# Key/value banks of a hybrid decoder block: one ScalarE copy ahead of the rest of the evacuation, and a later load of the feed-forward gate vector

## The chip, the core and the metric

The kernel runs on one core of a Trainium2 chip. TensorE (PE in the profile) multiplies matrices into PSUM banks of 128 x 512 single-precision numbers; VectorE (DVE), ScalarE (ACT) and GpSimd (POOL) do the rest. All transfers between the chip's memory and SBUF are issued by SyncE (SP), one after the other. Each engine runs its own instructions strictly in the order in which the program lists them, and waits for other engines at semaphores.

The metric is the device time of one execution in microseconds, the median of several runs. Before the change it is 2741.42 us (three runs, 2739.41 to 2742.02).

## The reference

One decoder layer on 2048 tokens of width 1024. Two mixers, sliding-window attention and a chunkwise mLSTM, work on one common projection, and a SwiGLU feed-forward part follows:

```python
h = modulate(rms_norm(x, g_pre_mix[l]), shift_m, scale_m)
proj = h @ w_in[l]
q_a, k_a, v_a, q_m, k_m, v_m, o_m, i_m, f_m, g_a, g_m = jnp.split(proj, split_points, axis=-1)
q_a = rope(q_a.reshape(B, S, N_Q_HEADS, HEAD_DIM), positions)      # 8 heads of 64
k_a = rope(k_a.reshape(B, S, N_KV_HEADS, HEAD_DIM), positions)     # 2 heads of 64
...
i_pre = i_m + b_if[l][:MLSTM_HEADS]                                # 4 and 4 columns
f_pre = f_m + b_if[l][MLSTM_HEADS:]
...
x = x + gate_m[:, None, :] * rms_norm(mix, g_post_mix[l])
h2 = modulate(rms_norm(x, g_pre_ffn[l]), shift_f, scale_f)
ff = (jax.nn.silu(h2 @ w_ffn_gate[l]) * (h2 @ w_ffn_up[l])) @ w_ffn_down[l]
x = x + gate_f[:, None, :] * rms_norm(ff, g_post_ffn[l])
```

`rope` turns each head's two halves of 32: `[t1*cos - t2*sin, t2*cos + t1*sin]`. The attention of a block of 128 queries sees its own 128 keys and the 128 before, so the kernel keeps, next to each token tile's values, their difference from the values of the tile before.

## The kernel before

**Blocks and stages.** The 2048 tokens are four blocks of 512 (`NBLK`), two blocks a superblock (`NSB`), four tiles of 128 tokens a block (`NT`). A superblock projects queries and keys/values of its first block (`q_kv(b0)`), the mLSTM values of both blocks (`vm(b0)`, `vm(b1)`), then `q_kv(b1)`; the other columns of the projection follow in pairs (`pair_parts`), with a scheme of seven instead of eight products. Attention and mLSTM run as streams beside these matmuls, and so do the preparation of the next block's h (`hprep`, `hsums`) and the modulation (`ada_stream`). After both superblocks' outputs comes the feed-forward part (`program2`): for each half of the tokens `gate_up`, then `down`.

**Precision.** Every product is made of three matmuls: weights and activations are split into a rounded part (a ScalarE cast, L259 or L1348) and a rest (a VectorE subtraction, L260 or L1349). So each part of the weights needs ScalarE, then VectorE, before TensorE can use it.

**Order.** The program text gives an order by priority, with streams interleaved by a clock that the program keeps itself (`now`, `spawn`, `tick`). The order on each engine is laid out when the program is built: it is opened with `schedule_with_timeline_sim=True`, so a scheduler plays through estimated times, issues on each engine what is ready, and gives out buffers as they come free. Once built, each engine's order is fixed.

**Banks and buffers.** The projections accumulate in `acc`, four banks. `token_group` takes all four at once, one per token tile, and calls `evac` for tile 0 to 3 as each one's last matmul is issued. A bank is free when the last instruction that reads it is done. The temporaries of the evacuations are tiles `tx`: nine buffers of one size, shared by rope, the modulation's loads, the convolutions and others.

**The query evacuation.** `rope` (L746 on) copies the bank into a `tx` tile on ScalarE (L751), multiplies by cosine and sine on VectorE (L759 to L761), then subtracts and adds (L762, L763). `q_stream` later transposes the result, splits it (L772, L773) and sends it to `at_d` in memory (L775).

**The key/value evacuation** (`evac_kv`, L800 on). The bank's 264 columns are 128 of keys, 128 of values, 8 of gates. VectorE adds the gate biases from the bank (L801, L802); ScalarE copies the values into `va` (L804); VectorE subtracts the last tile's values `v_last` from the bank (L805); ScalarE copies the new values into `v_last` (L806); SyncE sends both (L808, L810); then `rope` copies the keys from the bank (L751) and turns them, with its last add (L763) on GpSimd. `k_stream` transposes and splits the keys (L793, L794) and sends them to `at_d` (L797), from where the attention loads them (L898 to L903).

**The border.** The feed-forward part works in memory that the mixers gave back: `open_ffn` closes their pools and opens `fpool`. The first thing in `program2` is `load_gg` (L1809): it takes the first tile of that pool, 128 x 1024, and loads the gate vector `gg_f_d`, which `gated` multiplies with in `down` (L1652). Shortly after, `rest_of_hc` loads eight pieces of the feed-forward's h from `hc_d` (L1426) into tiles `w` and makes the rests of two operands of them (L1429). The last rows of `x` after the mixers leave by L579.

Of the kernel before, what the change touches and what calls it, by code (L numbers as in the profile page):

```python
# [10 lines left out]
F32 = mybir.dt.float32  # L11
# [4 lines left out]
ALU = mybir.AluOpType  # L16
# [3 lines left out]
P = 128  # L20
S = 2048
D = 1024
KD = D // P
TB = 512
NT = TB // P
# [6 lines left out]
HQ, HKV, HD = 8, 2, 64  # L32
# [39 lines left out]
def decoder_block(ctx: ExitStack, tc: tile.TileContext, a: dict, out: bass.AP, dbg=None):  # L72
    nc = tc.nc
    V, A, G, T = nc.vector, nc.scalar, nc.gpsimd, nc.tensor
# [18 lines left out]
    def nm(s):  # L93
        uid[0] += 1
        return f"{s}{uid[0]}"
# [4 lines left out]
    def mix_tile():  # L100
        return ps_mix.tile([P, 512], F32, tag="mix", name=nm("mix"))

    def tx(shape, dtype=F32):
        return tpool.tile(shape, dtype, tag="tx", name=nm("tx"), bufs=9)
# [48 lines left out]
    b_if = const.tile([P, 8], F32, name="b_if")  # L153
# [52 lines left out]
    def transpose(o, i):  # L206
        now[0] += 110.0
        k = i.shape[0]
        T.transpose(o, i, ident[:k, :k])  # L209

    def spawn(gen, delay=0.0):
        st = [now[0] + delay, gen, False]
        streams.append(st)
        return st
# [473 lines left out]
    AT_K, AT_V, AT_N = 2 * 512, 2 * 512 + 4 * P, 2 * 512 + 6 * P  # L688
# [12 lines left out]
    gt = kvp.tile([P, NT, 36], F32, name="gt")  # L701
    V.memset(gt, 0.0)
    v_last = kvp.tile([P, P], F32, name="v_last")
# [23 lines left out]
    at_d = [tc.dram_tile([P, AT_N], F32, name=f"at_d{i}") for i in range(S // P)]  # L727
# [8 lines left out]
    def superblock(sb):  # L736
        b0, b1 = 2 * sb, 2 * sb + 1
        R = {}
# [4 lines left out]
            return lhs  # L743


        def rope(ps, heads, b, t):  # L746
            sin, cos = tables[sb]
            t += (b % 2) * NT
            W = heads * HD
            raw = tx([P, W])  # L750
            A.copy(raw, ps[:, :W])  # L751
            src = raw.rearrange("p (h u f) -> p h u f", u=2, f=32)
            cb = cos[:, t, :].unsqueeze(1).to_broadcast([P, heads * 2, 32])
            sb_ = sin[:, t, :].unsqueeze(1).to_broadcast([P, heads, 32])
            y = tx([P, W])
            z = tx([P, W])
            zz = z.rearrange("p (h u f) -> p h u f", u=2, f=32)
            yy = y.rearrange("p (h u f) -> p h u f", u=2, f=32)
            V.tensor_tensor(y.rearrange("p (h f) -> p h f", f=32), raw.rearrange("p (h f) -> p h f", f=32), cb, op=ALU.mult)  # L759
            V.tensor_tensor(zz[:, :, 0, :], src[:, :, 1, :], sb_, op=ALU.mult)  # L760
            V.tensor_tensor(zz[:, :, 1, :], src[:, :, 0, :], sb_, op=ALU.mult)  # L761
            V.tensor_tensor(yy[:, :, 0, :], yy[:, :, 0, :], zz[:, :, 0, :], op=ALU.subtract)  # L762
            (G if heads == HKV else V).tensor_tensor(yy[:, :, 1, :], yy[:, :, 1, :], zz[:, :, 1, :], op=ALU.add)  # L763
            return y

        def q_stream(b, t, y):
            yield L_ROPE
            pt = mix_tile()
            for j in range(GQ):
                transpose(pt[:, j * P:(j + 1) * P], y[:, j * P:(j + 1) * P])  # L770
            hi, lo = tx([P, 512], F32R), tx([P, 512], F32R)
            A.activation(hi, pt, AF.Copy, scale=HD ** -0.5)  # L772
            V.scalar_tensor_tensor(lo, pt, HD ** -0.5, hi.bitcast(F32), op0=ALU.mult, op1=ALU.subtract)  # L773
            for i, q in enumerate((hi, lo)):
                nc.sync.dma_start(at_d[b * NT + t][:, i * 512:(i + 1) * 512], q.bitcast(F32))  # L775
# [1 line left out]
        R["qk"] = []  # L777

        def evac_q(b):
            return lambda t, ps: R["qk"].append(spawn(q_stream(b, t, rope(ps, HQ, b, t))))  # L780

        def load_kv():
            raw = raw_tile([KD, 264])
# [4 lines left out]
        def k_stream(n, y):  # L788
            yield L_ROPEK
            pt = mix_tile()  # L790
            transpose(pt[:, :P], y)
            kk = tx([P, 2, P], F32R)
            A.copy(kk[:, 0, :], pt[:, :P])  # L793
            V.tensor_tensor(kk[:, 1, :], pt[:, :P], kk[:, 0, :].bitcast(F32), op=ALU.subtract)  # L794
            for n_, u in ((n, 1), (n + 1, 0)):
                if n_ < S // P:
                    nc.sync.dma_start(at_d[n_][:, AT_K:AT_V].rearrange("p (i u k) -> p i u k", i=2, u=2)[:, :, u, :], kk.bitcast(F32))  # L797

        def evac_kv(b):
            def evac(t, ps):  # L800
                V.tensor_tensor(gt[:, t, 0:4], ps[:, 256:260], b_if[:, 0:4], op=ALU.add)  # L801
                V.tensor_tensor(gt[:, t, 32:36], ps[:, 260:264], b_if[:, 4:8], op=ALU.add)  # L802
                va = tx([P, 2, P])
                A.copy(va[:, 0, :], ps[:, 128:256])  # L804
                V.tensor_tensor(va[:, 1, :], ps[:, 128:256], v_last, op=ALU.subtract)  # L805
                A.copy(v_last, va[:, 0, :])  # L806
                n = b * NT + t
                nc.sync.dma_start(at_d[n][:, AT_V + P:], va[:, 1, :])  # L808
                if n + 1 < S // P:
                    nc.sync.dma_start(at_d[n + 1][:, AT_V:AT_V + P], va[:, 0, :])  # L810
                R["qk"].append(spawn(k_stream(b * NT + t, rope(ps, HKV, b, t))))
            return evac

        def q_kv(b):
# [516 lines left out]
    F = {}  # L1331
# [3 lines left out]
    def unit():  # L1335
        if "pool" not in F:
            return tm([P, TB])
        return F["pool"].tile([P, TB], F32, tag="w", name=nm("w"), bufs=16)
# [209 lines left out]
    def gate_up(b2):  # L1548
        late = None
        for p in range(NP):  # L1550
            g = {}

            def done_g(qd, t, in_psum, g=g):
                g[qd] = unit()
                A.activation(g[qd], t, AF.Sigmoid)
                V.tensor_tensor(g[qd], t, g[qd], op=ALU.mult)

            def done_u(qd, t, in_psum, p=p, g=g):
                V.tensor_tensor(g[qd], t, g[qd], op=ALU.mult)

                names = {"11": "11", "12": "21", "21": "12", "22": "22"}
                F["a", names[qd]] = g[qd]
                if qd != "12":
                    nc.sync.dma_start(as_d[b2][:, IDX[names[qd]], p, :], g[qd])
                    return
                g["all"] = {n: F.pop(("a", n)) for n in ("11", "12", "21", "22")}

            def a_sums(p=p, g=g):
                a_ = g["all"]
                s1_, s2_, s4_ = unit(), unit(), unit()  # L1570
                V.tensor_tensor(s1_, a_["21"], a_["22"], op=ALU.add)
                V.tensor_tensor(a_["21"], a_["11"], a_["21"], op=ALU.subtract)
                V.tensor_tensor(s2_, s1_, a_["11"], op=ALU.subtract)
                V.tensor_tensor(s4_, a_["12"], s2_, op=ALU.subtract)
                for n, t_ in (("S1", s1_), ("S3", a_["21"]), ("S2", s2_), ("S4", s4_)):
                    nc.sync.dma_start(as_d[b2][:, IDX[n], p, :], t_)

            gp, up = (list(pair_parts(w, p * 256, done, unit, unit, mix_tile)) for w, done in ((wg, done_g), (wu, done_u)))
            load, sums = down_weights(p)
            if F.get("late") is not None and p == 0:  # L1580
                def a_step():
                    if F["late"]:
                        F["late"].pop(0)()

                for part in gp + up:
                    part.after = a_step
            yield from gp[:2]
            if b2 + p == 0:
                yield lambda: rest_of_hc(0)
            if late:  # L1590
                yield late
            yield from gp[2:4]
            if b2 + p == 0:
                yield lambda: rest_of_hc(1)
            if b2 == 0:
                yield load
            yield from gp[4:] + up[:3]
            if b2 == 0:
                yield sums
            yield from up[3:]  # L1600
            late = a_sums
            if b2 == 0 and 1 <= p <= NT:
                yield lambda t=p - 1: norm_rows(NBLK - 1, t)
        yield late
# [193 lines left out]
    def program():  # L1798
# [7 lines left out]
        yield lambda: next(phase2)  # L1806
        yield from items[last:]

    def load_gg():  # L1809
        F["gg"] = F["pool"].tile([P, D], F32, name="gg_f")  # L1810
        nc.sync.dma_start(F["gg"], gg_f_d)

    def program2():
        yield load_gg
        for b2 in range(NB2):
            yield from gate_up(b2)
            yield from down(b2)

    phase2 = run2(program2())
    for _ in run2(program(), {i: lambda i=i: ada_raws.update({c0: load_ada(c0, n) for c0, n, _ in ADA[ADA_AHEAD[i - 1]:ADA_AHEAD[i]]}) for i in (1, 2)}):  # L1820
        pass
# [29 lines left out]
```

## Time and profile before

| | |
|---|---|
| median of 3 runs | 2741.42 us (2739.41 to 2742.02) |
| profiled execution | 2741.79 us, of which the span from the first to the last instruction is 2740.1 us |
| mean granted TensorE clock | 0.988 |
| VectorE busy | 1995.3 us (73%) |
| ScalarE busy | 1292.4 us (47%) |
| memory traffic | 513.99 MB, mean 188 GB/s |

In a list of waits, a row reads: engine and line that waited, after the arrow the engine and line it waited for, then the total, how often, and the longest. In a timeline a row gives start, duration, engine, line, operation, output and inputs, shapes and how many were merged; the bracket holds the idle time of the engine just before and what ended it. In the chain of waits, which is followed back from the last instruction, a row gives start, length and what ran. Tiles are named without their numbers: `acc` and `mix` are PSUM banks, `whi`, `wlo` and `hl` split weights, `big` large buffers. Busy time by stages, in us, around the four key/value projections:

```
stage (us)      TensorE busy   VectorE busy   granted clock
60 to 110           38.72          45.19          0.93
110 to 140          28.67          24.18          1.00
140 to 190          50.00          23.82          1.00
190 to 240          39.68          43.72          0.90
740 to 800          50.23          51.13          0.92
800 to 880          80.00          52.77          0.99
880 to 960          71.12          68.52          0.94
```

The four key/value projections end near 86, 208, 772 and 896 us.

### The profile page before, as it was taken

The numbers are of one execution on the slowest core, as the hardware profiler recorded it, in microseconds if no ns is written. First come the engines' busy times: TensorE is split into PE (matmuls) and PEld (weight loads), VectorE is DVE, ScalarE is ACT, GpSimd is POOL, SyncE is SP. The second block draws the span as 40 slices with busy tenths as digits, with TensorE's granted clock in tenths as the row PEclk, the third lists the DMA queues.
The fourth block names the chain that finished last, engine by engine and source line by source line (L and its number), as shares of the span: only waits on it lengthen the run. The fifth ranks groups of instructions, "written<-read, shape, count | busy, mean of one in ns | idle before, by whom it ended". The sixth has DMA issues, their size and how long they took to land.

```text
span 2740.1 us, 35791 instructions
## 1 busy us (share of the span) xinstructions
PE 2646.6 (97%) x12310; PEld 2139.0 (78%) x12310; DVE 1995.3 (73%) x3922; ACT 1292.4 (47%) x2542; POOL 158.6 (6%) x205
## 2 busy tenths in 40 slices
PE   6898999999989899999998999999999999999998
PEld 4666788888876668888887888888877888888886
DVE  7959877767785988876586767776677766766466
ACT  5646644445754564344563433334554333333444
POOL 2010002100101000110000000000000000000000
PEclk9999999999999999999999999999999999999999
DMA  6655445687674545568755654446675323324566
GB/s 247 232 173 166 139 142 174 212 330 257 218 239 126 199 154 159 185 219 304 255 195 197 198 179 161 147 157 204 208 261 192 116 98 102 108 97 141 183 214 215
DMA packets 355223, 513.99 MB, mean 188 GB/s; under 512 B 25297, under 2 KB 213837, under 8 KB 349921
## 3 DMA queue, kind: packets, MB, share of 16 engines
q1 hardware_dynamic: 355040, 511.71, 56.3%
q8 instruction: 97, 1.59, 0.2%
q14 instruction: 86, 0.70, 0.1%
HBM read 358.17 MB, written 145.06 MB: 184 GB/s over the span
## 4 chain that ended last, share of the span: by engine, by line
PE 80%; DVE 7%; DMA 6%; issue 4%; ACT 2%; SPq 0%; POOL 0%; DVEq 0%; POOLq 0%; ACTq 0%
PE acc L204 57%; PE mix L204 22%; PE mix L209 2%; DVE hl L1349 1%; DVE tm L428 1%; DMA raw<-in_w_ffn_down_dram 1%; DMA big<-big 1%; DMA tx<-in_w_ada_dram 1%; DMA big<-g_d 1%; ACT hl L1348 1%; DVE wlo L260 0%; DMA raw<-as_d 0%; DMA at<-at_d 0%; DMA big<-in_x_dram 0%; ACT tm L941 0%
## 5 line engine op out<-in xcount | busy, mean ns | idle before, releaser
L204 PE MATMUL acc<-big,hl 128*128 128x512 f32 x3936 | 949.5, 395 | 14.9 <-ACT tx L751 13.1
L204 PEld LDWEIGHTS acc<-big,hl 128*128 128x128 f32 x3936 | 735.8, 189 | 184.3 <-ACT tx L751 13.5
L1348 ACT CAST hl<-raw 128x512 fp32r<-128x512 f32 x732 | 440.2, 621 | 488.4 <-PE acc L204 226.7
L1349 DVE TENSOR_TENSOR hl<-raw,hl 128x512 fp32r<-128x512 f32 x732 | 497.9, 696 | 195.9 <-ACT hl L1348 195.4
L204 PE MATMUL acc<-whi,big 128*128 128x512 f32 (+1 forms) x1280 | 382.7, 378 | 22.8 <-ACT tx L751 15.0
L204 PE MATMUL mix<-big,hl 128*128 128x512 f32 x1232 | 334.0, 393 | 8.1 <-DVE big L1429 7.0
L204 PEld LDWEIGHTS acc<-whi,big 128*128 128x128 f32 x1280 | 234.9, 190 | 72.5 <-ACT tx L751 15.9
L204 PEld LDWEIGHTS mix<-big,hl 128*128 128x128 f32 x1232 | 231.7, 188 | 59.9 <-DVE big L1429 7.5
L204 PE MATMUL acc<-wlo,big 128*128 128x512 f32 (+1 forms) x640 | 240.6, 378 | 4.6 <-DVE wlo L260 4.5
L204 PE MATMUL acc<-hl,hl 128*128 128x512 f32 x1008 | 237.0, 393 | 4.3 <-DVE hl L1349 2.4
L204 PEld LDWEIGHTS acc<-hl,hl 128*128 128x128 f32 x1008 | 187.0, 188 | 49.6 <-DVE hl L1349 7.9
L204 PE MATMUL mix<-hl,hl 128*128 128x512 f32 x792 | 183.2, 391 | 2.4 <-ACT hl L1348 1.6
L204 PEld LDWEIGHTS mix<-hl,hl 128*128 128x128 f32 x792 | 147.9, 188 | 36.8 <-ACT hl L1348 3.5
L260 DVE TENSOR_TENSOR wlo<-raw,whi 128x1024 fp32r<-128x1024 f32 (+1 forms) x96 | 110.3, 1149 | 76.1 <-ACT whi L259 70.1
L204 PE MATMUL acc<-big,whi 128*128 128x512 f32 x512 | 155.0, 391 | 1.2 <-ACT whi L259 1.2
L259 ACT CAST whi<-raw 128x1024 fp32r<-128x1024 f32 (+1 forms) x96 | 94.3, 984 | 120.6 <-PE acc L204 116.1
L204 PEld LDWEIGHTS acc<-wlo,big 128*128 128x128 f32 x640 | 122.7, 192 | 28.1 <-DVE wlo L260 6.2
L475 POOL TENSOR_TENSOR rs<-ms,nhalf 128x1 f32<-128x1 f32 (+1 forms) x56 | 42.1, 764 | 1650.6 <-DVE ms L473 1518.7
L204 PE MATMUL acc<-hcT2h,hl 128*128 128x512 f32 x352 | 118.1, 396 | 1.5 <-ACT w L1492 1.5
L204 PE MATMUL mix<-hcT4h,hl 128*128 128x512 f32 x352 | 117.3, 394 | 0.0
L204 PEld LDWEIGHTS acc<-big,whi 128*128 128x128 f32 x512 | 95.6, 188 | 21.2 <-ACT whi L259 1.7
L204 PE MATMUL acc<-big,wlo 128*128 128x512 f32 x256 | 96.4, 392 | 0.1
(333 smaller groups left out, 3392.7 us busy)
## 6 DMA issues: line engine op xcount, KB each, us to landing
raw<-in_w_in_dram SPq DMA_DIRECT2D x48, 1024.0 KB
as_d<-w SPq DMA_DIRECT2D x154, 256.0 KB
raw<-as_d SPq DMA_DIRECT2D x70, 512.0 KB
raw<-in_w_ffn_gate_dram SPq DMA_DIRECT2D x22, 1024.0 KB
raw<-in_w_ffn_up_dram SPq DMA_DIRECT2D x22, 1024.0 KB
raw<-ws_d SPq DMA_DIRECT2D x40, 512.0 KB
tx<-in_w_ada_dram SPq DMA_DIRECT2D x64, 256.0 KB
y_d<-tm SPq DMA_DIRECT2D x64, 256.0 KB
```

The costliest lines, as they stand in the source:

```text
L204: T.matmul(o, lhsT=lhsT, rhs=rhs, start=start, stop=stop, skip_group_check=resumed)
L209: T.transpose(o, i, ident[:k, :k])
L259: A.copy(hv, src)
L260: V.tensor_tensor(lv, src, hv.bitcast(F32), op=ALU.subtract)
L428: V.scalar_tensor_tensor(acc, raw[:, k, :], c_, acc, op0=ALU.mult, op1=ALU.add)
L475: G.tensor_tensor(r[:, :n], ms[:, :n], nhalf[:, :n], op=ALU.pow)
L1348: A.copy(v(hi), src)
L1349: V.tensor_tensor(v(lo), src, v(hi).bitcast(F32), op=ALU.subtract)
```

## The change

In the key/value evacuation one ScalarE copy takes all 264 columns of the bank into a `tx` tile, now 392 columns wide. Everything else reads that tile: rope the keys, VectorE the values (the difference goes into columns 264 to 391) and the gate columns. The order becomes rope, difference, `v_last` (now a VectorE copy), gate additions. Both transfers leave from that one tile, so a token tile takes four `tx` buffers (this one, two of rope, one of `k_stream`) instead of five. Rope's last addition is on VectorE for keys too. The query evacuation makes the same copy as before, outside `rope`.

In the feed-forward part the place of the gate vector is still taken first, by `place_gg`; its load is issued after the first `gate_up`, ahead of the first `down`.

```diff
-        def rope(ps, heads, b, t):
+        def rope(raw, heads, b, t):
             sin, cos = tables[sb]
             t += (b % 2) * NT
             W = heads * HD
-            raw = tx([P, W])
-            A.copy(raw, ps[:, :W])
+            raw = raw[:, :W]
...
-            (G if heads == HKV else V).tensor_tensor(yy[:, :, 1, :], yy[:, :, 1, :], zz[:, :, 1, :], op=ALU.add)
+            V.tensor_tensor(yy[:, :, 1, :], yy[:, :, 1, :], zz[:, :, 1, :], op=ALU.add)
             return y
...
         def evac_q(b):
-            return lambda t, ps: R["qk"].append(spawn(q_stream(b, t, rope(ps, HQ, b, t))))
+            def evac(t, ps):
+                raw = tx([P, 512])
+                A.copy(raw, ps)
+                R["qk"].append(spawn(q_stream(b, t, rope(raw, HQ, b, t))))
+            return evac
...
         def evac_kv(b):
             def evac(t, ps):
-                V.tensor_tensor(gt[:, t, 0:4], ps[:, 256:260], b_if[:, 0:4], op=ALU.add)
-                V.tensor_tensor(gt[:, t, 32:36], ps[:, 260:264], b_if[:, 4:8], op=ALU.add)
-                va = tx([P, 2, P])
-                A.copy(va[:, 0, :], ps[:, 128:256])
-                V.tensor_tensor(va[:, 1, :], ps[:, 128:256], v_last, op=ALU.subtract)
-                A.copy(v_last, va[:, 0, :])
+                raw = tx([P, 392])
+                A.copy(raw[:, :264], ps[:, :264])
+                v, dv = raw[:, 128:256], raw[:, 264:392]
                 n = b * NT + t
-                nc.sync.dma_start(at_d[n][:, AT_V + P:], va[:, 1, :])
+                y = rope(raw, HKV, b, t)
+                V.tensor_tensor(dv, v, v_last, op=ALU.subtract)
+                V.tensor_copy(v_last, v)
+                V.tensor_tensor(gt[:, t, 0:4], raw[:, 256:260], b_if[:, 0:4], op=ALU.add)
+                V.tensor_tensor(gt[:, t, 32:36], raw[:, 260:264], b_if[:, 4:8], op=ALU.add)
+                nc.sync.dma_start(at_d[n][:, AT_V + P:], dv)
                 if n + 1 < S // P:
-                    nc.sync.dma_start(at_d[n + 1][:, AT_V:AT_V + P], va[:, 0, :])
-                R["qk"].append(spawn(k_stream(b * NT + t, rope(ps, HKV, b, t))))
+                    nc.sync.dma_start(at_d[n + 1][:, AT_V:AT_V + P], v)
+                R["qk"].append(spawn(k_stream(n, y)))
             return evac
...
-    def load_gg():
+    def place_gg():
         F["gg"] = F["pool"].tile([P, D], F32, name="gg_f")
+
+    def load_gg():
         nc.sync.dma_start(F["gg"], gg_f_d)
 
     def program2():
-        yield load_gg
+        yield place_gg
         for b2 in range(NB2):
             yield from gate_up(b2)
+            if b2 == 0:
+                yield load_gg
             yield from down(b2)
```

More of the change, by code (lines that the diff above doesn't have):

```diff
@@ L1807, in program @@
         yield from items[last:]
+    def place_gg():
+        F["gg"] = F["pool"].tile([P, D], F32, name="gg_f")
     def load_gg():
-        F["gg"] = F["pool"].tile([P, D], F32, name="gg_f")
         nc.sync.dma_start(F["gg"], gg_f_d)
     def program2():
-        yield load_gg
+        yield place_gg
         for b2 in range(NB2):
             yield from gate_up(b2)
+            if b2 == 0:
+                yield load_gg
             yield from down(b2)
```

## The prediction, made before the result was known

> **What bounds the kernel now.** I read the busy times of the page first, then the list of waits for TensorE alone, then the timeline of TensorE around each of the long waits.
>
> ```profile
> PE 2646.6 (97%) x12310; PEld 2139.0 (78%) x12310; DVE 1995.3 (73%) x3922; ACT 1292.4 (47%) x2542; POOL 158.6 (6%) x205
> ```
>
> TensorE works in 2646.6 of 2740.1 us, so whatever shortens the program must come out of the 93.5 us in which it stands, or out of stretches in which it works slowly. The waits (total, times, longest):
>
> ```profile
> PE acc L204 <- ACT tx L751: 28.0, 5, 8.6
> ...
> PE mix L204 <- DVE big L1429: 7.0, 1, 7.0
> ...
> PE acc L204 <- DVE wlo L260: 4.5, 3, 2.1
> ```
>
> The first is the copy at L751 that empties a PSUM bank. The timeline (start, duration, then in brackets the idle time and who ended it) shows where:
>
> ```profile
> 94.63 0.80 PE L204 MATMUL acc<-whi,big 128*128 128x512 f32 x1 [8.55 <-ACT tx L751]
> ...
> 216.49 4.96 PE L204 MATMUL acc<-big,hl 128*128 128x512 f32 x12 [8.34 <-ACT tx L751]
> ...
> 221.32 2.98 PE L204 MATMUL acc<-big,hl 128*128 128x512 f32 x12
> ...
> 760.86 0.39 PE L204 MATMUL acc<-whi,big 128*128 128x264 f32 x1 [2.54 <-ACT tx L751]
> ...
> 780.86 0.79 PE L204 MATMUL acc<-whi,big 128*128 128x512 f32 x1 [3.90 <-ACT tx L751]
> ...
> 900.55 4.35 PE L204 MATMUL acc<-big,hl 128*128 128x512 f32 x12 [4.71 <-ACT tx L751]
> ```
>
> Four of the five (8.55, 8.34, 3.90, 4.71; together 25.5) stand at the end of the key/value projection of one block of 512 tokens: it fills all four banks of the pool, and the next projection can't start until a bank is free. The fifth (2.54) is a query bank, which the change leaves as it is. There is a second price: after such a wait 12 matmuls take 4.96 or 4.35 instead of 2.98, a tail of 1.98 or 1.37 us in which the array runs slowly. After 3.90 the first matmul is slow too (0.79), after 2.54 it is not (0.39).
>
> Why the bank is held so long is told by the chain of waits that ended last (start, length, what):
>
> ```profile
> 93.88 0.21 DVE tx L805
> ...
> 94.12 0.30 ACT v_last L806
> 94.42 0.17 ACT tx L751
> ...
> 94.63 7.23 PE acc L204 x24
> ```
>
> ScalarE does L804, L806, L751 in this order. L806 must wait for the subtraction at L805, and VectorE gets to that late. The bank is free only after the last of them, though ScalarE's first read of it came much earlier:
>
> ```profile
> 89.62 0.29 ACT L804 COPY tx<-acc 128x128 f32<-128x128 f32 x1
> ...
> 211.58 0.26 ACT L804 COPY tx<-acc 128x128 f32<-128x128 f32 x1
> ...
> 774.63 0.28 ACT L804 COPY tx<-acc 128x128 f32<-128x128 f32 x1
> ...
> 895.99 0.25 ACT L804 COPY tx<-acc 128x128 f32<-128x128 f32 x1
> ```
>
> **The change, part by part: the single copy.** It takes the place of L804 as the first ScalarE instruction of a tile and frees the bank alone. No row shows a copy of 264 columns; the nearest are 128 and 512:
>
> ```profile
> L751 ACT COPY tx<-acc 128x512 f32<-128x512 f32 x16 | 9.0, 591 | 10.4 <-DVE tx L761 6.7 <-issue 3.4 <-PE acc L204 0.2
> ...
> L804 ACT COPY tx<-acc 128x128 f32<-128x128 f32 x16 | 4.2, 265 | 2.7 <-DMA at_d<-tx 2.5 <-DVE tx L761 0.2
> ```
>
> On the line between them it is 265 + (136/384) x 326 = 380 ns (bounds 265 and 591). I leave it at L804's time, because what stands ahead of L804 on ScalarE (casts and the h tiles) isn't touched, and add 0.04 us to the matmul. New starts: 89.62 + 0.42 = 90.04, against 94.63: 4.6 gained. 211.58 + 0.42 = 212.0, against 216.49: 4.5. At 775.05 TensorE is still at its transposes (they end at 780.86 - 3.90 = 776.96), so all 3.9 go. 895.99 + 0.42 = 896.4 against 900.55: 4.1. Sum 17.1. The wait of the third vanishes and that of the fourth falls to 0.6, so their slow tails go too: 1.4 each by the 900.55 row, 2.8. The first two still stand 3.96 and 3.85 us, as long as the 3.90 that was slow; I leave their tails. Gain so far 19.9. Bounds: the copies come no earlier than L751 does now (0), or as soon as the bank is full (25.5 and all four tails).
>
> The Trainium skill ("TensorE: Matmul & The Clock Gate", section "What's actually happening") says that about 3.4 us without work halve the clock until the array has been busy as long again. The 2.54 and the 3.90 above agree; by its window half a microsecond less of the first two waits would save some 3 us more.
>
> **What VectorE takes over.** Per tile it gets the add of L763 from POOL and the copy of `v_last` from ScalarE; the two gate adds and the subtraction only change their source.
>
> ```profile
> L805 DVE TENSOR_TENSOR tx<-acc,v_last 128x128 f32<-128x128 f32 x16 | 4.5, 284 | 0.6 <-ACT tx L804 0.6
> ...
> L1122 DVE COPY tx<-hist 128x3 f32<-128x3 f32 x21 | 4.0, 197 | 0.0
> L762 DVE TENSOR_TENSOR tx<-tx,tx 128x64 f32<-128x64 f32 x16 | 3.8, 236 | 0.0
> ```
>
> The add is as L762, 236 ns of which some 90 overlap the neighbour; the copy lies between 197 (three columns) and 284. About 0.3 us a tile, 1.2 a block. That would be free where VectorE has room, but it has none here (columns: window, width, PE, PEld, DVE, ACT, POOL, clock, DMA, GB/s):
>
> ```profile
> 90.00:100.00 10.00, 5.37 (x17) 4.32 (x18) 9.93 (x33) 4.82 (x13) 1.15 (x2) 0.66 0.70 239
> ...
> 210.00:220.00 10.00, 3.51 (x8) 2.81 (x9) 10.00 (x27) 4.77 (x12) 0.70 (x1) 0.52 0.78 253
> ```
>
> I charge the first two blocks 1.2 each, 2.4. In return rope no longer stands behind L751. Rope's five instructions and the gate adds now wait for one copy; behind the gate adds stand only the gates (L830 on), needed much later by the mLSTM.
>
> **What is late next.** TensorE comes earlier to work whose inputs hang on transfers (chain of waits again):
>
> ```profile
> 109.85 7.16 DMA tx<-in_w_ada_dram
> ...
> 125.74 5.23 DMA tx<-in_w_ada_dram
> ...
> 898.50 8.75 DMA big<-big
> ...
> 911.56 2.57 PE acc L204 x10
> ```
>
> Between 110 and 131 (125.74 + 5.23) the chain goes through loads for the modulation, whose times TensorE doesn't set: I take half of the first block's 4.6 back, 2.3 (bounds 0 and 4.6). In the fourth the sums T1 and T3 land at 907.25 (898.50 + 8.75) whatever TensorE does, and it needed split weights behind them at 911.56: 2.0 back of 5.5. The bank copies are worth 19.9 - 2.4 - 2.3 - 2.0 = 13.2.
>
> **The gate vector.** The chain at the border to the feed-forward part, and what SyncE issued there:
>
> ```profile
> 1440.27 4.38 DMA x<-tm
> ...
> 1444.66 0.32 SPq L1811
> ...
> 1445.04 4.55 DMA w<-hc_d
> ...
> 1450.36 2.93 PE mix L204 x6
> ```
>
> ```profile
> 1440.87 0.38 SPq L1515 DMA_DIRECT2D raw<-in_w_ffn_gate_dram  x1
> ```
>
> The load at L1811 goes into memory that the last `x` rows still leave, waits 3.3 us for that, and behind it on SyncE's queue stand the eight loads of `hc_d` for which L1429 and then TensorE wait (7.03). Without it the first may issue at 1441.3 instead of 1445.04: 3.7 earlier at best. It then meets the weight load issued at 1440.87. Sizes:
>
> ```profile
> raw<-in_w_ffn_gate_dram SPq DMA_DIRECT2D x1, 1024.0 KB
> w<-hc_d SPq DMA_DIRECT2D x8, 256.0 KB
> ...
> gg_f<-gg_f_d SPq DMA_DIRECT2D x1, 512.0 KB
> ```
>
> Now 512 + 256 KB take from 1444.66 to 1449.59, 4.93; if 1024 + 256 KB took that pace from 1440.87, the load would land at 1449.1, 0.5 earlier. I take 2.0 between 0.5 and 3.7 (0 if its own buffer waits for the same rows). The moved load costs SyncE 0.32 us and one transfer at the start of the down projection, near 1838; its first reader comes at 1996.5, so it is hidden by 150 us of matmuls:
>
> ```profile
> L1625 SPq DMA_DIRECT2D raw<-as_d x84: 319/320/456, 1838.1 to 2717.0; - x84
> ```
> ```profile
> L1652 DVE TENSOR_TENSOR w<-w,gg_f x24: 679/684/693, 1996.5 to 2705.5; 128x512 f32<-128x512 f32 x24
> ```
>
> The Trainium skill ("DMA: Bandwidth & Descriptors", section "Issuing engines are not separate DMA queues") has all transfers share the same 16 engines, which speaks for the 0.5; by that the sum would be 1.5 worse.
>
> **Sum.** 13.2 + 2.0 = 15.2. The profiled execution took 2741.79 (2740.1 of it span), the median of the runs is 2741.42, 0.4 below. 2741.8 - 15.2 - 0.4 = 2726.
>
> **Rivals.** First, the copies move up to where the banks fill. For it: a tile now needs four `tx` buffers instead of five, so a copy may find one sooner; against it: ScalarE was busy with earlier work until 89.6. All 25.5, four tails (1.98 + 3 x 1.4 = 6.2) and 3.7 at the border: 35.4, giving 2706.
>
> Second, the gain is given back: VectorE was full and stays the bound, TensorE starts sooner and stands later at the split weights and attention loads. For it speaks that the chain into 94.63 is VectorE work; against it, that TensorE waits for split weights (L260) 4.5 us in all today. Only the third block's 3.9 + 1.4 less 2.4 is left, and nothing at the border: 2738.5.
>
> Third, slower: the copy of the fourth tile takes the buffer of the first, which is held until two transfers from it have landed, and ScalarE, in order, stands on it with the weight casts behind. Such a transfer has taken
>
> ```profile
> 778.70 6.69 DMA at_d<-tx
> ```
>
> At the first block: VectorE reaches tile 0 at 93.9, has rope and difference (six instructions of some 0.2) done at about 95.2, the buffer comes at 101.9. TensorE, started at 90.04 with a tail of 2, has used the three free banks (18 matmuls of 2.98/12 us) by 96.5: it stands 5.4 and pays a tail of 1.8 again, 7.2 against 4.6 gained. Four times 2.6, plus 2.4, less 2.0 at the border: 10.8 slower, 2752. It decides once that copy comes later than about 99. Against it: nine buffers, four tiles of them needed at once, and only 2.5 us of L804 waiting for such a transfer today.
>
> That the change doesn't do what it says would be L804's place slipping: the order on each engine is laid out at build time from estimated times, so the new copy can be put behind other casts. That ends as the second rival.
>
> **How the numbers follow.** Forecast 0.47, more gain 0.18, given back 0.20, slower 0.15. No change means within 0.2%, 5.5 us, about what a measurement of this kernel can tell: 2735.9 to 2746.9. Of "given back" 0.05 falls below, 0.13 inside, 0.02 above; of "slower" 0.04 inside, since it need not strike all four blocks. Faster 0.47 + 0.18 + 0.05 = 0.70, same 0.17, slower 0.13. The range runs from 2706 to 2746, which leaves out most of the slower case and the tip of the first; the forecast's own is 2718 (nothing charged or taken back, 3.7 at the border) to 2734 (half of 15.2).
>
> **What would show it.** TensorE's waits for the key/value copy down to some 8 us in all and near 90, 212 and 896, none at 776; the copy in 0.38; no wait of ScalarE for VectorE in the evacuation; the wait at the border near 5 us. Wrong would be: waits of the same size behind split weights, `at_d` or `big<-big` a few us later (second rival), or ScalarE standing on `tx` before the fourth copy (third).

## The result, and the profile after the change

| kernel | median, us | runs | ratio to the kernel before, 95% interval |
|---|---|---|---|
| before | 2743.14 | 8 | |
| after the change | 2733.48 | 8 | 0.9962 [0.9952, 0.9971] |

The change is faster by 0.38% of 2743, 10.4 us; the two profiled executions have spans of 2740.1 and 2729.8, 10.3 apart. The forecast was 15.2 faster. The kernel before has five more runs here than ahead of the prediction, so its median is 2743.14 where it was 2741.42.

The profile after, first the busy times of the page, then the list of TensorE's waits (total us, times, longest):

```profile
PE 2641.6 (97%) x12310; PEld 2133.7 (78%) x12310; DVE 1999.4 (73%) x3954; ACT 1287.9 (47%) x2510; POOL 153.2 (6%) x189
```
```profile
PE acc L204 <- ACT tx L805: 9.8, 6, 4.2
...
PE acc L204 <- DVE hl L1354: 6.9, 7, 1.9
PE mix L204 <- DVE big L1434: 6.0, 1, 6.0
...
PE acc L204 <- ACT w L1497: 4.4, 4, 1.3
PE acc L204 <- DVE wlo L260: 4.1, 3, 2.2
PE acc L204 <- ACT tx L781: 4.0, 3, 2.2
PE acc L204 <- ACT tx L827: 3.4, 3, 1.9
```

L805 is the new copy, L781 the query copy that was part of L751. Together they cost TensorE 13.8 us where L751 cost 28.0, so 14.2 of waiting went. The busy time fell by 5.0 (2646.6 to 2641.6), the slow matmuls after the long waits. But other waits grew. L1354 (the rests of split operands, L1349 before) went from 2.8 to 6.9, L1497 (the copy of a bank in the feed-forward part, L1492 before) from 1.5 to 4.4, and L827 (the copy of a bank with mLSTM values) is new with 3.4. From the list of before:

```profile
PE acc L204 <- DVE hl L1349: 2.8, 4, 1.1
...
PE acc L204 <- ACT w L1492: 1.5, 2, 1.0
```

The wait at the border to the feed-forward part (L1434, L1429 before) fell by 1.0.

Where the 10.3 came from is seen by setting the n-th matmul of one trace beside the n-th of the other; both have 12310. Inside a stage their order differs, so the difference means something only where both traces are in step again, as from 300 to 740, where it stays the same:

```
time in the trace before, us    300   740  1000  1440  1475  1700   end
after the change, us earlier    3.0   3.0  13.1  12.5  14.0  10.5  10.3
```

The first superblock (8.55 and 8.34 us of waiting before) yields 3.0, the second 9.5 to 10, the border 1.5; between 1475 and 1700, in a part that the change doesn't touch, 3.5 are lost.

TensorE after each of the four key/value stages (timeline: start, duration, then idle time and who ended it):

```profile
90.97 0.50 PE L204 MATMUL acc<-whi,big 128*128 128x512 f32 x1 [1.47 <-ACT tx L805]
...
209.47 4.59 PE L204 MATMUL acc<-big,hl 128*128 128x512 f32 x12 [4.16 <-ACT tx L805]
...
215.09 3.04 PE L204 MATMUL acc<-big,hl 128*128 128x512 f32 x12 [1.02 <-ACT tx L805]
...
782.41 0.50 PE L204 MATMUL acc<-whi,big 128*128 128x512 f32 x1 [1.55 <-ACT tx L805]
...
889.46 5.94 PE L204 MATMUL acc<-big,hl 128*128 128x512 f32 x23 [1.31 <-ACT tx L805]
```

Three of the four long waits shrink to some 1.5 us; the second, 8.34 before, still has 4.16, and 12 matmuls behind it still take 4.59 in place of 3.04. ScalarE's timeline tells why (same columns):

```profile
84.03 0.67 ACT L805 COPY tx<-acc 128x264 f32<-128x264 f32 x2
...
90.53 0.38 ACT L805 COPY tx<-acc 128x264 f32<-128x264 f32 x1 [0.55 <-DMA at_d<-tx]
...
94.30 0.38 ACT L805 COPY tx<-acc 128x264 f32<-128x264 f32 x1 [3.39 <-DVE tx L762]
...
202.88 2.18 ACT L551 CAST big<-big 128x512 fp32r<-128x512 f32 x4 [4.22 <-DMA big<-big]
...
206.97 2.17 ACT L551 CAST big<-big 128x512 fp32r<-128x512 f32 x4
209.04 0.38 ACT L805 COPY tx<-acc 128x264 f32<-128x264 f32 x1
214.65 0.38 ACT L805 COPY tx<-acc 128x264 f32<-128x264 f32 x1 [5.24 <-DMA at_d<-tx]
```

In the first block two copies run at 84.0, 5.6 us ahead of L804's old 89.62, before TensorE needs a bank. In the second, casts of the sums T2 and T4, which land at 202.88, stand ahead of the copy, and the next copy stands 5.24 us on a `tx` buffer that a transfer still reads. The view of the copy's own line:

```profile
L805 ACT COPY tx<-acc x16: 376/380/409, 84.0 to 895.5; 128x264 f32<-128x264 f32 x16
...
  DMA at_d<-tx: 11.9, 4
```

It takes 380 ns, and ScalarE stood 11.9 us, four times, until such a transfer had landed. It also stood 9.6 us, six times, until VectorE was done (L762 3.6, L760 3.1, L1449 2.7, L426 0.2).

The border, SyncE's queue first, then the chain of waits:

```profile
1428.33 0.38 SPq L1520 DMA_DIRECT2D raw<-in_w_ffn_gate_dram  x1
1429.05 0.42 SPq L1818 DMA_DIRECT2D gg_f<-gg_f_d  x1
1429.53 5.99 SPq L1431 DMA_DIRECT2D w<-hc_d  x8
```
```profile
1427.07 1.97 DMA x<-tm
...
1429.53 6.45 DMA w<-hc_d
```

The gate vector's load (L1818) is still issued ahead of the eight `hc_d` loads and behind the last rows. The source calls it after the gate/up part; the order of the queue, laid out at build time, has it where it was. Something else changed there: the rows that it waits for landed in 1.97 us (4.38 before), so the eight loads were issued 1.20 us behind the weights and not 4.17. But the first of them then took 6.45 us in place of 4.55. It landed 7.65 us after the weights' issue, 8.72 before, so that of 3.0 us on the queue 1.1 were left.

### The profile page after: what moved, and what is told of

Same layout as the page of the kernel before. It is cut to its first block, busy times and chain, and to the rows that moved or that the text cites. A ratio compares the mean times of both kernels' runs of the same rounds, so it can differ in the third digit from the quotient of the medians.

```text
span 2729.8 us, 35753 instructions
## 1 busy us (share of the span) xinstructions
PE 2641.6 (97%) x12310; PEld 2133.7 (78%) x12310; DVE 1999.4 (73%) x3954; ACT 1287.9 (47%) x2510; POOL 153.2 (6%) x189
## 4 chain that ended last, share of the span: by engine, by line
PE 75%; DVE 8%; DMA 4%; issue 4%; ACT 2%; POOL 0%; SPq 0%; DVEq 0%; POOLq 0%; ACTq 0%
PE acc L204 53%; PE mix L204 21%; DVE hl L1354 2%; PE mix L209 1%; DMA w<-x 1%; ACT hl L1353 1%; DMA raw<-as_d 1%; DMA at_d<-tx 1%; DVE tx L1132 1%; DMA raw<-in_w_ffn_down_dram 0%; DMA tx<-in_w_ada_dram 0%; DVE tx L578 0%; DVE big L1354 0%; DMA w<-hc_d 0%; POOL rs L475 0%
## 5 line engine op out<-in xcount | busy, mean ns | idle before, releaser
L1354 DVE TENSOR_TENSOR hl<-raw,hl 128x512 fp32r<-128x512 f32 x732 | 497.7, 696 | 193.0 <-ACT hl L1353 192.3
L260 DVE TENSOR_TENSOR wlo<-raw,whi 128x1024 fp32r<-128x1024 f32 (+1 forms) x96 | 109.3, 1138 | 73.0 <-ACT whi L259 66.6
```

What stands on the lines that cost most here:

```text
L260: V.tensor_tensor(lv, src, hv.bitcast(F32), op=ALU.subtract)
L1354: V.tensor_tensor(v(lo), src, v(hi).bitcast(F32), op=ALU.subtract)
```

## Experiments

All are timed in five rounds against the kernel before on the same chip. The ratios are to that kernel; the changed kernel's 0.9962 is the mark.

**The two parts, each alone.** The copies alone: the changed kernel with

```
         yield place_gg
+        yield load_gg
...
-            if b2 == 0:
-                yield load_gg
```

> The copy part alone; the gate vector's load stands in the program where it stood before. Theory: in the trace after the change the load of the gate vector is still issued ahead of the eight loads of hc_d (1429.05 against 1429.53), so the second edit did nothing at the border and the whole gain belongs to the copies: ratio to the kernel before 0.996, as after the change, within 1.5 us of 2733.5. Rival (the prediction's sum, border 2.0): some 2 us slower than the changed kernel.

Measured: 2731.43, ratio 0.9959 [0.9944, 0.9974].

The gate vector alone: the kernel before with `place_gg` and the late `load_gg` of the diff.

> The second edit alone, on the kernel before. Theory: the order on the queue at the border stays as it was, so no change, ratio 1.000 within 0.0006. Rival (the prediction's term for the border): 2.0 us faster, between 0.5 and 3.7, ratio 0.9993.

Measured: 2741.24 against 2742.55, ratio 0.9990 [0.9981, 0.9998], between theory and rival. Its queue at the border keeps the order of before: weights at 1441.81, the gate vector at 1445.53, `hc_d` at 1445.90. What else would make it faster isn't known. Since the kernel without the edit is as fast as the one with it, the gain is that of the copies.

**The load truly late.** The changed kernel with the load held behind what was written ahead of it:

```
-        nc.sync.dma_start(F["gg"], gg_f_d)
+        tc.keep_in_program_order(nc.sync.dma_start(F["gg"], gg_f_d))
```

> The changed kernel with the gate vector's load held behind everything that the gate/up part issues, so that it truly comes late. Theory: 512 KB fewer ahead of the hc_d loads, which now land 6.45 us after their issue; at the 400 GB/s or so that the busiest slices show these are 1.3 us, and the issue can come up to 0.8 earlier: 1.3 to 2.1 us faster than the changed kernel, TensorE's wait at the border 4 to 4.7 in place of 6.0. Rival: the hc_d loads hang on the rows that leave, whatever stands ahead: 0.

Measured: 2728.93, ratio 0.9946 [0.9934, 0.9958]. Its queue, chain and wait:

```profile
1430.91 0.38 SPq L1520 DMA_DIRECT2D raw<-in_w_ffn_gate_dram  x1
1431.39 5.49 SPq L1431 DMA_DIRECT2D w<-hc_d  x8
```
```profile
1431.39 5.76 DMA w<-hc_d
```
```profile
PE mix L204 <- DVE big L1434: 4.5, 1, 4.5
```

From the issue of the weights to the landing of the first `hc_d` load it is 6.2 us (1431.39 + 5.76 - 1430.91); in the changed kernel it was 7.65. The wait is 1.5 shorter, as expected. So in this pair of profiles the edit's idea has a gain; the edit as written didn't carry it out. The whole time moved by more (4.5 between medians), but the intervals overlap.

**The new wait in the gate/up part.** In the changed kernel between 1500 and 1515, chain of waits:

```profile
1500.46 5.59 DMA ws_d<-big
...
1506.20 0.38 SPq L1530
...
1507.14 6.04 DMA w<-x
...
1513.93 0.48 ACT w L1497
...
1514.45 2.60 PE acc L204 x10
```

A load of down weights (L1530) stands on SyncE until the transfers out of its buffer have landed; behind it stands the second half of an `x` row (L1548), ScalarE stands on that half, and the copy L1497 of a full bank is next on ScalarE. This was close in the kernel before too (one wait of 0.5). The experiment puts the row first:

```
-            nc.sync.dma_start(xr, x1[blk][t * P:(t + 1) * P, c])
+            F["row"] = nc.sync.dma_start(xr, x1[blk][t * P:(t + 1) * P, c])
...
+            with (tc.issue_after(F["row"].ins) if "row" in F else ExitStack()):
                 nc.sync.dma_start(st["raw"], wdn[p * 256:(p + 1) * 256, :]...
```

> The changed kernel with each load of down weights in the feed-forward part held behind the two row loads of the late norm. Theory: the 3.5 us that the changed kernel loses between 1500 and 1650 come from the second row load, which stands on SyncE's queue behind a load of down weights that waits for the ws_d transfers; ScalarE stands on that row with the copy of a full bank behind it, three times 1.0 to 1.3. With the rows first these waits go: 3.5 us faster than the changed kernel, ratio to the kernel before 0.995. Rival: the rows land late for want of bandwidth or of a buffer, or the down weights come late instead: no gain or a loss.

Measured: 2726.24, ratio 0.9938 [0.9925, 0.9951], faster than the changed kernel and the one before. Busy time from 1500 to 1660, first of the changed kernel, then of this one (columns: window, width, PE, PEld, DVE, ACT, POOL, clock, DMA, GB/s), and its queue:

```profile
1500.00:1660.00 160.00, 156.60 (x682) 127.47 (x681) 115.61 (x196) 63.37 (x121) 2.16 (x4) 1.00 0.55 180
```
```profile
1500.00:1660.00 160.00, 160.00 (x701) 131.28 (x700) 121.79 (x203) 65.70 (x123) 2.17 (x4) 1.00 0.60 202
```
```profile
1502.77 0.44 SPq L1549 DMA_DIRECT2D w<-x  x1
...
1505.17 0.42 SPq L1549 DMA_DIRECT2D w<-x  x1
1505.68 0.42 SPq L1531 DMA_DIRECT2D big<-in_w_ffn_down_dram  x1
```

TensorE works without a gap, 3.4 us more than in the changed kernel; the two profiled spans (2729.8 and 2726.2) are 3.6 apart.

Being ahead isn't shown to be what makes these waits. Between 1475 and 1700 us TensorE stands for this copy 3.4 us in the changed kernel, 1.7 with the copies alone and 2.3 with the load held back, but also 2.2 with the second edit alone, a kernel that is 0.9 behind the kernel before at 1440. With the rows first nothing is left. So the place of the row load makes the waits possible, and how much of them one execution pays doesn't follow from the lead. Both remedies in one kernel:

> The changed kernel with the gate vector's load held back and the late rows' loads first, both. Theory: the two act at different places (1430 and 1500 to 1650) and add up: 1.4 to 2.4 at the border and 3.5 behind it, ratio to the kernel before 0.992 to 0.994. Rival: the gate/up part gives the border's gain back: no better than the rows alone, 0.9938.

Measured: 2727.91, ratio 0.9936 [0.9923, 0.9950]. It can't be told from the rows alone. The profile says that little was to be had: TensorE waits 5.2 us at the border where it waits 5.8 with the rows first alone, so that holding the load back saves 0.6 here and not 1.5, and both profiled spans are 2726.2.

**One read, or no wait of ScalarE.** The kernel before had two faults in one place: five reads of a bank by two engines, and ScalarE's copy of `v_last` waiting for VectorE. One kernel mends the second alone, on the kernel before:

```
-                A.copy(v_last, va[:, 0, :])
+                V.tensor_copy(v_last, va[:, 0, :])
```

> The kernel before, with the copy of v_last on VectorE alone; ScalarE no longer waits for VectorE between its two reads of a bank, but the bank is still read five ways. Theory: the bank comes free with the last read, and VectorE's subtraction reads it until 94.1, the last ScalarE copy ended at 94.6: at most 0.5 to 1 us a block, ratio to the kernel before 0.9985 to 1.000. Rival: the order of ScalarE's wait was the cause: most of the gain of the change, 0.997.

The other brings it back in the changed kernel:

```
-                V.tensor_copy(v_last, v)
+                A.copy(v_last, v)
```

> The changed kernel with the copy of v_last on ScalarE again, which waits there for VectorE's subtraction. Theory: the first bank is still freed by one copy, but the copies of the next tiles stand behind a copy that waits for VectorE: half of the gain is left, 0.9975 to 0.999 of the kernel before. Rival: one read of the bank is all that counts: 0.996, as after the change.

Measured: 2750.70, ratio 1.0027 [1.0018, 1.0036], and 2731.84, ratio 0.9953 [0.9940, 0.9966]. What ScalarE stood on, in the first kernel ahead of its last read of the bank (L751), in the second ahead of the copy of `v_last` (L810):

```profile
  DVE tx L805: 13.6, 8
```
```profile
L810 ACT COPY v_last<-tx x16: 283/299/318, 92.5 to 905.6; 128x128 f32<-128x128 f32 x16
...
  DVE tx L809: 10.0, 8
```

Why the first is slower than the kernel before isn't settled: TensorE's waits for L751 fell from 28.0 to 23.3, but those for split weights (L260) grew from 4.5 to 7.2 and those for L1492 from 1.5 to 6.3. That it gains nothing is the point. With `v_last` on VectorE, L751 itself waits for the subtraction L805, though neither reads what the other writes; all they share is the bank. With `v_last` on ScalarE, ScalarE stands 10.0 us for VectorE and the kernel is by its median as fast as the changed one. (Its profiled execution, the slowest of its five, leads by only 6.5 at 1440 us, so a cost of a few us isn't excluded there.) So one read by one engine makes the gain, and the theory of the second run (half the gain lost) was wrong. The change also put rope ahead of the difference; that order alone wasn't tried. The Trainium skill ("PSUM — Partial Sum Buffer", section "PSUM bank collisions raise a hardware error") says that two engines mustn't access one bank at once, reads included, so that a wait goes between them; the 13.6 us agree. No run here let the two read at once.

**What VectorE took over.**

```
-            V.tensor_tensor(yy[:, :, 1, :], yy...
+            (G if heads == HKV else V).tensor_tensor(yy[:, :, 1, :], yy...
```

> The changed kernel with the last add of rope for key tiles on GpSimd again. Theory of the prediction: VectorE is full in these stretches and each of its instructions there is charged; without this add (236 ns a tile) up to 1 us faster than the changed kernel. Rival: VectorE's extra work lies beside other work: 0, or up to 1 slower since the GpSimd add took 374 ns and up to 1372 and the key's transpose waits for it.

Measured: 2734.39, ratio 0.9962 [0.9949, 0.9976], the changed kernel's. The add costs nothing that these runs can measure, on either engine.

**What takes the first superblock's gain back.** Three runs looked for it. First, the buffers on which ScalarE stands:

```
-            y = tx([P, W])
-            z = tx([P, W])
+            if heads == HKV:
+                yz = tx([P, 2, W])
+                y, z = yz[:, 0, :], yz[:, 1, :]
+            else:
+                y = tx([P, W])
+                z = tx([P, W])
```

> The changed kernel with the two rope tiles of a key tile in one tx buffer: three tx buffers a key/value tile in place of four. Theory: in the changed kernel ScalarE stands 11.9 us in all (four times, 5.24 the longest) ahead of the key/value copies until a transfer out of a tx buffer (at_d<-tx) has landed, and TensorE's longest wait for the copy (4.2 near 209) comes from that; with fewer buffers in use it goes: TensorE's waits for the copy 5 us or less in place of 9.8, 2 to 5 us faster than the changed kernel. Rival: the stand moves to the next tile that needs a buffer, or the time is given back at the loads behind: 0.

Measured: 2731.89, ratio 0.9951 [0.9937, 0.9966]. The stand ahead of the copy (L809 here) hardly shrank, and TensorE's waits moved to the split weights:

```profile
  DMA at_d<-tx: 10.2, 6
```
```profile
PE acc L204 <- DVE wlo L260: 9.4, 5, 3.2
...
PE acc L204 <- ACT tx L809: 5.8, 2, 4.5
```

Second, the loads that the prediction had named, left out of both kernels:

```
-                    raw = tx([P, 1, 512])
-                    nc.sync.dma_start(raw, w_ada[:, c0:c0 + 512]...)
+                    if k == 0 or part != 2:
+                        raw = tx([P, 1, 512])
+                        nc.sync.dma_start(raw, w_ada[:, c0:c0 + 512]...)
+                    else:
+                        raw = acc.unsqueeze(1)
```

> The changed kernel without 14 of the 16 loads of w_ada that the first superblock issues for the mixer's gate (256 KB each); the terms are added from the accumulator in their place, so VectorE's work stays and the gate isn't the reference's. Theory of the prediction (its step of 2.3 us given back to these loads): the changed kernel enters the second key/value stage 9.9 us ahead and leaves it 2.5 ahead because these loads and what waits behind them set the pace; without them the lead at 300 us over the kernel before grows from 3 to 7 or more, and the distance to the kernel before without the same loads (next run) grows from 10 to 14 or more. Rival: VectorE, at 19 of 20 us busy between 220 and 240, or the sums T2 and T4 set that pace: the distance stays 10 within 2.

> The kernel before without the same 14 loads, the pair to the run above; the gate isn't the reference's here either. Theory: TensorE's long waits for the bank copy at 95 and 216 stay (8.6 and 8.3), since VectorE's lateness and not a load makes them: 0 to 3 us faster than the kernel before. Rival: the loads made these waits: 5 us or more.

Measured: 2724.15, ratio 0.9922 [0.9910, 0.9935], and 2739.09, ratio 0.9976 [0.9967, 0.9985]. The medians are 14.9 apart, which the theory had asked for, but the two intervals leave that some 4 us uncertain, and the two profiled spans (2723.8 and 2735.7) are 11.9 apart. The place speaks against it: at 300 us the first leads the second by 1.5, not by 7. Without the loads the long waits of the kernel before stay, too:

```profile
PE acc L204 <- ACT tx L754: 25.2, 5, 7.4
```

Third, the casts ahead of the second block's copy, put behind it (on the rows-first kernel):

```
-        yield L_HD
+        yield L_HD if names[0] != "T2" else 1e9
...
+                with (tc.issue_after(F["kvc"].ins) if names[0] == "T2" else ExitStack()):
                     A.copy(hi[:, k, :], v)
...
+                c_ = A.copy(raw[:, :264], ps[:, :264])
+                if t == 0:
+                    F["kvc"] = c_
```

> The kernel of the rows-first run, with the casts of the sums T2 and T4 issued behind the first key/value copy of the second block of each superblock. Theory: in the changed kernel that bank is full at 205.3 and its copy runs at 209.04, since ScalarE stands in order on casts of sums that land at 202.88; TensorE waits 4.2 us there, which is what is left of the 8.3. With the copy first TensorE starts again near 206, 3.5 us earlier, and 1 to 3.5 us of that reach the end: ratio to the kernel before 0.9925 to 0.9935, against 0.9938 without it. Rival: the products that follow wait for these casts and VectorE's part of them, and the lead is given back by 300 us, as the rest of the first superblock's gain was: 0.994, or slower.

Measured: 2758.94, ratio 1.0056 [1.0042, 1.0071], slower. TensorE's timeline:

```profile
207.34 4.61 PE L204 MATMUL acc<-big,hl 128*128 128x512 f32 x12 [2.92 <-ACT tx L806]
...
933.28 1.87 PE L204 MATMUL mix<-ones,tm 128*128 128x1 f32 x8 [14.33 <-DVE tm L428]
...
941.95 2.07 PE L204 MATMUL mix<-tm,ones 128*128 128x512 f32 x2 [6.80 <-DVE tm L466]
```

TensorE does start earlier, at 207.34 (210.22 in the rows-first kernel, 209.47 in the changed one), and by 300 us is 7.6 behind the rows-first kernel. In the second superblock it stands 14.3 and 6.8 us for modulation terms, which come late: in the chain there two loads of them take 4.56 and 7.37 us ahead of VectorE's L428. The edit shifted more than the casts, so it says only that this start alone isn't what the first superblock lacks.

What the traces show of that superblock is a spread. TensorE's waits from 60 to 300 us in the changed kernel:

```profile
PE acc L204 <- ACT tx L805: 7.0, 4, 4.2
PE acc L204 <- DVE wlo L260: 4.1, 3, 2.2
PE mix L209 <- POOL tm L950: 2.3, 3, 1.2
PE acc L204 <- ACT tx L781: 1.8, 2, 1.2
PE acc L204 <- ACT tx L827: 1.6, 2, 1.1
PE acc L204 <- ACT hl L1353: 1.0, 1, 1.0
```

Before, L751 stood here with 16.9 and all others together with 5.8 (the whole list has 22.7). Now L805 has 7.0 and the others, with four smaller ones not shown, 13.0. Of 9.9 gained, 7.2 went to waits of about a microsecond behind ScalarE, VectorE and GpSimd. Which of them would have to go first stays open.

## The prediction, step by step

- **The copy's price**, 380 ns by the line between two rows: measured 380.
- **The copy in L804's place.** Right in the second superblock: 8.8 forecast there (3.9 + 4.1 + two tails of 1.4 less 2.0 taken back), 9.5 to 10 measured, though 1.55 of the third block's wait stayed where none was to. Too cautious in the first block: the copies came at 84.03, not 89.6, which is the first rival's mechanism, and the wait was 1.47 where 3.96 was to stay. In the second block L804's place held: the wait was 4.16, 3.85 by the sum, and it ended at 209.47 and not 212.0 because TensorE got there 2.8 earlier.
- **The tail after 2.54.** The row at 760.86 (0.39) was taken as not slow beside matmuls of 512 columns, but it has 264, and its neighbours take 0.28. It was 0.11 slow, as the first matmul after 1.47 us is (0.50 against 0.39). The granted clock bears out the reading all the same: 1.00 from 758 to 764 us, 0.51 from 777 to 784, after the 3.90.
- **Why the bank was held.** The prediction blamed ScalarE's order (L806 waiting for L805). The runs show that L751 waits for L805 without L806, and that, once the bank is free, the wait for VectorE costs nothing that shows in the medians. The forecast of one reader freeing the bank stands on the right part of the change for half the right reason.
- **VectorE's charge, 2.4.** The add, half of it, measured as nothing. The copy of `v_last` on ScalarE instead changed nothing in the median either.
- **Given back in the first block, 2.3, to the modulation loads.** The loads aren't shown as the cause, and it was too little: the first superblock kept 3.0 where the sum had 4.4 (4.6 + 4.5 - 2.4 - 2.3), though it had gained more on the way, and without the loads the lead at 300 us is no larger. Here the second rival was right that the gain is given back. Of its two places the split weights took 1.1 more (4.1 us of waits, 3.0 before) and the attention loads nothing; the rest went to waits that it hadn't named.
- **All bank copies, 13.2:** 12.5 by 1440 us in the profiled execution, 9.7 to 11.3 in four other kernels with the same copies (the copies alone, load held back, rows first, both remedies). That the whole came so near is in part luck: too much in the first superblock stood against too little in the second.
- **The border, 2.0.** This step failed: "Without it the first may issue at 1441.3 instead of 1445.04". The load was not gone from there. I took the place in the source for the place in the queue, with the warning in my own text that the order is laid out at build time. The 1.5 gained there came with the copies alone too (9.7 to 11.1), so that it lies near the 2.0 is luck. The lower bound was well argued: the `hc_d` loads did come to be issued 3.0 us sooner, and 1.1 of it was left.
- **Missing from the sum: -3.5 in the gate/up part.** "What is late next" was asked of the stages around the copies, not of this one, where the trace before already had a wait of half a microsecond. That the place of the row load makes the loss possible is shown by the rows-first run; that the lead makes it is not.
- **The third rival**'s mechanism is there (11.9 us of ScalarE standing on buffers, 5.24 longest), but the copy in question came at 94.30, ahead of its threshold of 99.
- **The signs.** The waits for the copy came to 9.8 where some 8 was named, the wait at the border to 6.0 where 5 was. That ScalarE wouldn't wait for VectorE in the evacuation was wrong (9.6 us).

So 13.2 + 2.0 became about 12.5 + 1.5 - 3.5 = 10.5: direction and main term right, the gain a third smaller than forecast, most of it lost in a stage that the prediction didn't look at.

## What to carry to other kernels

Empty a PSUM bank with one instruction of one engine and let all further work read the copy; here, with the reads split over two engines, ScalarE's read waited for VectorE's though they touch different columns. Before counting on a moved load, look at the queue in the trace: here the order was laid out at build time, the place in the source didn't move the load, and a stated dependence did. And when TensorE is to get ahead by ten microseconds, look in every stage behind for waits that are already there and may take some of it.

## What had not been expected

Kernels with nearly the same instructions in the first 1400 us (the changed one, load held back, rows first) led the kernel before by 12.5, 10.0 and 10.9 us at 1440. A single profile therefore places a gain to about 2 us, and terms of 1 or 2 us can be told only by a wait that is gone from the list, not by the time of arrival. Even a wait moves: at the border it was 6.0, 5.8 and 2.9 us in three kernels with the gate vector's load in the same place (the changed one, the copies alone, `v_last` on ScalarE).
